# Second layer norm of a decoder layer: one early shift of all rows, VectorE takes the sums in a fixed order

## Chip, cores and metric

One core of one Trainium2 chip runs the whole kernel. The metric is device time in microseconds, from launch to end, median of three runs.

## The reference, cut to what matters

One layer of a hybrid decoder for 1024 prompt rows and 8 sample rows, 1032 rows of 1024 channels in all. The change lies in the last two lines, the feed-forward part and the layer norm behind it:

```python
x = layer_norm(ALPHA * x + (1 + g1) * m, ln1_g, ln1_b)
v = x * (1 + sc2) + sh2
hid = jnp.square(jax.nn.relu(v @ w_up))                      # 1024 -> 4096
x = layer_norm(ALPHA * x + (1 + g2) * (hid @ w_down), ln2_g, ln2_b)

def layer_norm(x, g, b):
    mu = x.mean(-1); var = ((x - mu) ** 2).mean(-1)
    return (x - mu) * rsqrt(var + LN_EPS) * g + b
```

## The kernel before, in words

Activations lie transposed: channels on the 128 partitions, in 8 row groups m = 0 to 7 (`x1[0]` to `x1[7]`), and the 1032 sequence positions along the columns. A layer norm therefore sums over partitions and over the 8 tiles. The sum over partitions is a matmul with a matrix of ones (`total`, L814 to L821), whose result stands on every partition and is evicted by ScalarE (ACT).

**Matmuls.** Every fp32 operand is split into a high and a low part (`split`, L202: ACT casts the high part, VectorE (DVE) subtracts for the low part). A `product` (L217) is, for each block of columns, three matmuls (L210: high x high, low x high, high x low) per 128 channels of the contraction, into one of four PSUM banks of tag mm, and then an evacuation by VectorE. The weight loads go through SP's queue (L146) into two buffers of tag raw, one weight ahead of use.

**Feed-forward.** The 4096 hidden channels are done in 5 chunks of four and then NFB = 2 chunks of six groups of 128. Each chunk first makes its hidden groups (`hidden`, L907 to L925): 24 matmuls per block of 344 columns, then per block ACT's relu, VectorE's square (L919), ACT's copy to the high part (L919) and VectorE's low part (L920). Then eight products with w_down are added into `x1[m]` by VectorE (`gate_add`, L761 to L768: one operation from PSUM, and for the block that holds the sample rows two narrow ones over 8 columns). All hidden groups read the same eight operand pairs `vh[k]`, `vl[k]`, which are the tiles `ks`; pair k = 4 was made with the tags ("xg", "xg") (L692), and tag xg has two buffers (L52). Pair 0 holds the two buffers of tag yc.

**Last chunk.** Its eight products run by column blocks LAST (L62): columns 640 to 1032, 256 to 640, 0 to 256. While the products of one block run, `ln2` takes the sums of the rows of that block: for row 0 a base is taken (its mean over 128 channels, L799 and L817), every row is shifted by it on VectorE (L825), squared on ACT (L806), the squares are summed on GpSimd (POOL, L810) and the rows on VectorE (L811). `finish` makes mean and variance (L837 to L851: two sums on PE, ln, exp and square on ACT, a Newton step on VectorE). The block before gets its output meanwhile: the shift by the mean on POOL (L825), the product with the reciprocal deviation on VectorE (L829), gain and bias on ACT (L986) or, for m = 3 to 5, on POOL (L984), and a DMA (L987). The last block's output has its own lines (L1024 to L1032).

**What sets the order.** A scheduler lays down each engine's instructions in one fixed sequence when the program is built. It takes what is ready by its own timing, and a new tile of a tag gets its buffer when all that reads the old tile in that buffer is done. Inside `manual_schedule` the instructions of the engines named keep the order in which they are written. Before, that holds for VectorE in the last block, and for VectorE and ACT behind it.

Of the kernel before, what the change touches and what calls it, by code (L numbers as in the profile page):

```python
# [11 lines left out]
F32R = mybir.dt.float32r  # L12
AF = mybir.ActivationFunctionType
ALU = mybir.AluOpType
# [3 lines left out]
P = 128  # L18
D = 1024
# [22 lines left out]
V_G2 = V_B1 + 8  # L42
V_B2 = V_G2 + 8
# [4 lines left out]
M_SH1, M_SC1, M_G1, M_SH2, M_SC2, M_G2 = (8 * i for i in range(6))  # L48
# [6 lines left out]
NFB = 2  # L55
# [4 lines left out]
BLOCKS = [(b * BW, (b + 1) * BW) for b in range(NB)]  # L60
LATER = [BLOCKS[2], BLOCKS[0], BLOCKS[1]]
LAST = [(640, T), (256, 640), (0, 256)]  # L62


def cols(ap, b):
    return ap[:, b[0]:b[1]]


def build(tc, ctx, a):
    nc = tc.nc  # L70
    dma = nc.sync.dma_start
    act = nc.scalar.activation
    ts = nc.vector.tensor_scalar
    tt = nc.vector.tensor_tensor
    stt = nc.vector.scalar_tensor_tensor
# [10 lines left out]
    def nm(s):  # L86
        uid[0] += 1
        return f"{s}_{uid[0]}"

    def slab(tag, dt=F32):  # L90
        return sp.tile([P, T], dt, tag=tag, name=nm(tag), bufs=SLOTS.get(tag, 1))

    def tmp(w=T, dt=F32):
        return sp.tile([P, w], dt, tag="t", name=nm("t"), bufs=5)

    def psm():
        return pm.tile([P, 512], F32, tag="mm", name=nm("mm"))

    def psa():
        return pq.tile([P, 512], F32, tag="ada", name=nm("ada"), bufs=1)  # L100

    def pss():
        return pq.tile([P, 512], F32, tag="sm", name=nm("sm"))
# [12 lines left out]
    eps = cp.tile([P, 1], F32, tag="eps", name="eps")  # L116
# [20 lines left out]
    def vc(base, j):  # L137
        return vec[:, base + j:base + j + 1]
# [49 lines left out]
    def prefetch():  # L188
        if order:
            key, raw = load_next()  # L190
            ahead.append((key, parts(*raw)))

    def weights(*key):
        if not ahead:
            prefetch()
        got, w = ahead.pop(0)
        assert got == key, (got, key)
        prefetch()
        return w
# [4 lines left out]
    def term(ps, w, x, i, n, b, which=range(3)):  # L204

        ko, xh, xl = x
        w_h, w_l = (t[:, ko * P:(ko + 1) * P] for t in w)
        for q in which:
            wt, xt = ((w_h, xh), (w_l, xh), (w_h, xl))[q]
            mm(ps[:, :b[1] - b[0]], wt, cols(xt, b), start=(i == 0 and q == 0), stop=(i == n - 1 and q == 2))  # L210

    def product(w, ks, evac, blocks=BLOCKS):
        for b in blocks:
            ps = psm()
            for i, x in enumerate(ks):
                term(ps, w, x, i, len(ks), b)
            evac(b, ps[:, :b[1] - b[0]])  # L217
            if not quiet[0]:
                next(background, None)
# [77 lines left out]
    with tc.manual_schedule(engines={mybir.EngineType.PE, mybir.EngineType.DVE, mybir.EngineType.Activation}):  # L297
        for q in range(4):
            ps = psa()
# [21 lines left out]
            for j, x in zip(js, xin):  # L321
                s, b = mod[:, M_SC1 + j], mod[:, M_SH1 + j]
# [3 lines left out]
                last = [nc.scalar.copy(uh[j], x)]  # L326
# [70 lines left out]
    for i in range(2):  # L397
        t, w, body, tail = pair0[i]
# [252 lines left out]
    def gated(j):  # L651
        gc = tmp()
        project(8 + j, lambda b, ps: nc.scalar.copy(cols(gc, b), ps))
        t, w, body, tail = padded(3)
        project(16 + j, lambda b, ps: tt(cols(body, b), ps, cols(gc, b), op=ALU.mult))
        r = convolve(t, w, 3, tail, sct4[:, j], lambda k: vc(V_CONVW + 8 * k, j), ncp[:, j], sct4[:, j])
        y = slab("yc")
        project(j, lambda b, ps: tt(cols(y, b), ps, cols(r, b), op=ALU.mult))
        return y
# [13 lines left out]
    y = gated(0)  # L673
    pre = ssd_pre(0)
    for c in range(NC):
# [7 lines left out]
        y = y1  # L683
# [22 lines left out]
    sums = []  # L706
    for g in range(2):
        for j in range(4 * g, 4 * g + 4):
# [9 lines left out]
            x, sq = xs[j][:, :TP], sz[:, :TP]  # L718
# [29 lines left out]
    x1 = [slab(f"U{m}") for m in range(8)]  # L748
    rones = cp.tile([P, P], F32R, tag="low", name="rones")
# [11 lines left out]
    def gate_add(dst, ps, row, m, b):  # L761

        lo, hi = b[0], min(b[1], TP)
        stt(dst[:, lo:hi], ps[:, :hi - lo], mod[:, row + m, 0:1], dst[:, lo:hi], op0=ALU.mult, op1=ALU.add)  # L764
        if b[1] > TP:
            gs = sp.tile([P, NS], F32, tag="gs", name=nm("gs"))
            tt(gs, ps[:, hi - lo:], mod[:, row + m, 1:9], op=ALU.mult)
            tt(dst[:, TP:T], dst[:, TP:T], gs, op=ALU.add)  # L768
# [18 lines left out]
    class Norm:  # L787
# [26 lines left out]
        def total(self, dst, srcs, n, b, bias=None, w=ones):  # L814
            pn = pss()[:, :b[1] - b[0]]
            for i, src in enumerate(srcs):
                mm(pn, w, src, start=(i == 0), stop=(i == len(srcs) - 1))  # L817
            if bias is None:
                act(cols(dst, b), pn, AF.Copy, scale=1.0 / n)
            else:  # L820
                act(cols(dst, b), pn, AF.Identity, scale=1.0 / n, bias=bias)  # L821
# [43 lines left out]
    ln1 = Norm(x1, ("st", "U14", "U15"))  # L865
# [58 lines left out]
    def hidden(i):  # L924
        w, evac, hl, _ = hidden_start(i)  # L925
        product(w, kv, evac)
        return hl
# [32 lines left out]
    for f in range(NFA):  # L960
        kh = [t[2] for t in two] if f == 0 else []
        kh += [hidden(4 * f + i) for i in range(len(kh), 4)]
        for mp in range(4):
            w = weights("wda", f, mp)
            for m in (2 * mp, 2 * mp + 1):
                product(w, [(4 * (m % 2) + i, h, l) for i, (h, l) in enumerate(kh)],
                        lambda b, ps: gate_add(x1[m], ps, M_G2, m, b))
    for f in range(NFB):
        kh = [hidden(4 * NFA + 6 * f + i) for i in range(6)]
        kf = [(i, h, l) for i, (h, l) in enumerate(kh)]  # L970
        if f < NFB - 1:
            for m in range(8):
                product(weights("wdb", f, m), kf, lambda b, ps: gate_add(x1[m], ps, M_G2, m, b))
            continue
        ln2 = Norm(x1, ("xg", "xg", "yc"))

        def output_start(m, b):
            ln2.shift(m, b, nc.gpsimd)
            ln2.scale(m, b)

        def output_end(m, b):
            x = cols(x1[m], b)
            if 2 < m < 6:
                nc.gpsimd.tensor_scalar(x, x, vc(V_G2, m), vc(V_B2, m), op0=ALU.mult, op1=ALU.add)  # L984
            else:
                act(x, x, AF.Identity, scale=vc(V_G2, m), bias=vc(V_B2, m))  # L986
            dma(a["o_y"][m, :, b[0]:b[1]], x)  # L987

        def output(m, b):
            output_start(m, b)  # L990
            output_end(m, b)

        wd = []

        def last_block(i):
            b, last = LAST[i], i == len(LAST) - 1
            for m in range(8):
                if i == 0:
                    wd.append(weights("wdb", f, m))
                product(wd[m], kf, lambda b, ps: gate_add(x1[m], ps, M_G2, m, b), (b,))  # L1000
                for k in ((), (0,), (1, 2))[m] if m < 3 else (m,):
                    ln2.add(k, b, last)
                if i and 2 < m < 6:
                    output(m - 3, LAST[i - 1])
            if not last:
                ln2.finish(b)
            if i:
                for m in range(3, 8):
                    output_start(m, LAST[i - 1])
                    if not last or m < 6:  # L1010
                        output_end(m, LAST[i - 1])

        for i in range(len(LAST) - 1):
            last_block(i)
        with tc.manual_schedule(engines={mybir.EngineType.DVE}):
            last_block(len(LAST) - 1)
        b = LAST[-1]
        w = b[1] - b[0]
        y = [tmp(4 * w).rearrange("p (m c) -> p m c", m=4) for i in range(2)]
        with tc.manual_schedule(engines={mybir.EngineType.DVE, mybir.EngineType.Activation}):  # L1020
            ln2.finish(b, (range(4), ()), range(4, 8), lambda: [output_end(m, LAST[-2]) for m in (6, 7)])
            for m in range(8):
                x, to = cols(x1[m], b), y[m // 4][:, m % 4]
                ln2.scale(m, b, nc.gpsimd if m > 5 else nc.vector)  # L1024
                if m > 5:
                    nc.gpsimd.tensor_scalar(to, x, vc(V_G2, m), vc(V_B2, m), op0=ALU.mult, op1=ALU.add)
                elif m == 3:
                    ts(to, x, vc(V_G2, m), vc(V_B2, m), op0=ALU.mult, op1=ALU.add)
                else:
                    act(to, x, AF.Identity, scale=vc(V_G2, m), bias=vc(V_B2, m))  # L1030
                if m % 2:
                    dma(a["o_y"][m - 1:m + 1, :, b[0]:b[1]].rearrange("m p c -> p m c"), y[m // 4][:, m % 4 - 1:m % 4 + 1])  # L1032

# [80 lines left out]
```

## Time and profile before

| | |
|---|---|
| median of three runs | 1598.09 us (1596.28 to 1599.17) |
| profiled execution, its own time | 1595.34 us |
| its span in the profile | 1593.6 us |
| mean granted clock | 0.992 |
| last feed-forward chunk's products | from 1497.72 us to 1572 us |

Times within the profile are microseconds from the span's start. PE is the matrix engine, DVE is VectorE, ACT ScalarE, POOL GpSimd. A row of the timeline gives start, length, engine, line of the code, operation, output and inputs, shape and count, and in brackets how long the engine was idle before and what ended that. Several instructions in a row of the same kind are merged; the lengths of neighbours overlap a little, as an operation's start is reported before the one ahead of it is through.

### The profile page before, as it was taken

Reading aid. Unit: us, or ns where it says so; the run is one execution under the profiler, and the core shown is the slowest. Engines: PE = TensorE matmul, PEld = TensorE weight load, DVE = VectorE, ACT = ScalarE, POOL = GpSimd, SP = SyncE. Lnnn points to the kernel's source line nnn. Section 1 sums busy time; section 2 is a strip of 40 time slices with the busy share of each in tenths; the row PEclk is TensorE's granted clock in tenths of the full one; section 3 lists DMA queues with packets and bytes.
Section 4 is the critical chain, followed back from the end, with each engine's and each line's share of the span. In section 5 each row is a group of like instructions: output and inputs, shape, how many; then the busy total and the mean of one; then the engine's idle time right before and its main releaser. Section 6 shows DMA issues by size and latency. Waiting matters only on the chain.

```text
span 1593.6 us, 24010 instructions
## 1 busy us (share of the span) xinstructions
PE 1545.2 (97%) x10057; PEld 1492.0 (94%) x10057; DVE 877.3 (55%) x1629; ACT 524.2 (33%) x803; POOL 214.1 (13%) x212
## 2 busy tenths in 40 slices
PE   7999979999999999999999999999999999999994
PEld 4899878999999999999999999999999999999994
DVE  4576556767666652545897434434343433333488
ACT  2453322333333343713477122121312113113334
POOL 0017880000000001100241000000000000000076
PEclk9999989999999999999999999999999999999998
DMA  9434443333333322512311111111111111111211
GB/s 362 124 110 135 150 162 113 120 120 119 120 106 104 111 104 70 200 53 66 106 58 62 41 40 54 41 53 41 53 42 52 42 52 43 41 54 46 70 41 66
DMA packets 49628, 141.44 MB, mean 89 GB/s; under 512 B 5736, under 2 KB 14696, under 8 KB 49520
## 3 DMA queue, kind: packets, MB, share of 16 engines
q1 hardware_dynamic: 49520, 139.91, 26.8%
q8 instruction: 79, 1.29, 0.3%
q14 instruction: 29, 0.24, 0.1%
HBM read 126.33 MB, written 13.56 MB: 88 GB/s over the span
## 4 chain that ended last, share of the span: by engine, by line
PE 85%; DVE 5%; POOL 5%; DMA 2%; issue 1%; ACT 1%; SPq 0%; ACTq 0%; DVEq 0%; POOLq 0%
PE mm L210 78%; POOL s L526 1%; PE ada L229 1%; POOL w L528 1%; POOL w L525 1%; PE sm L626 1%; PE sm L618 1%; DMA s<-in_ssm 1%; DVE U L825 1%; POOL s L523 1%; PE sm L613 1%; PE sm L817 1%; PE sm L648 1%; DVE U L829 1%; DMA o_ssm<-s 1%
## 5 line engine op out<-in xcount | busy, mean ns | idle before, releaser
L210 PE MATMUL mm<-U,whi 128*128 128x344 f32 x3058 | 780.5, 324 | 0.0
L210 PEld LDWEIGHTS mm<-U,whi 128*128 128x128 f32 x3058 | 538.8, 189 | 17.7 <-issue 13.6
L210 PE MATMUL mm<-U,wlo 128*128 128x344 f32 x1529 | 490.1, 323 | 0.0
L202 ACT CAST whi<-raw 128x1024 fp32r<-128x1024 f32 (+1 forms) x124 | 127.6, 1030 | 525.7 <-PE mm L210 517.5
L210 PEld LDWEIGHTS mm<-U,wlo 128*128 128x128 f32 x1529 | 288.1, 189 | 3.1 <-issue 2.9
L764 DVE SCALAR_TENSOR_TENSOR U<-mm,mod,U 128x344 f32<-128x344 f32 (+3 forms) x216 | 122.5, 570 | 203.4 <-PE mm L210 203.3
L210 PE MATMUL mm<-S,whi 128*128 128x344 f32 (+3 forms) x912 | 233.0, 320 | 0.0
L202 DVE TENSOR_TENSOR wlo<-raw,whi 128x1024 fp32r<-128x1024 f32 (+1 forms) x124 | 150.9, 1217 | 127.2 <-ACT whi L202 126.8
L210 PEld LDWEIGHTS mm<-S,whi 128*128 128x128 f32 x912 | 160.6, 188 | 0.1
L210 PE MATMUL mm<-S,wlo 128*128 128x344 f32 (+3 forms) x456 | 145.0, 319 | 0.0
L210 PE MATMUL mm<-C,whi 128*128 128x344 f32 x516 | 143.0, 320 | 0.0
L810 POOL TENSOR_TENSOR yc<-yc,t 128x392 f32<-128x392 f32 (+2 forms) x20 | 21.2, 1062 | 681.2 <-ACT t L806 680.7
L919 DVE TENSOR_TENSOR t<-t 128x344 f32<-128x344 f32 x96 | 49.3, 515 | 93.6 <-ACT t L919 93.6
L210 PEld LDWEIGHTS mm<-C,whi 128*128 128x128 f32 x516 | 92.9, 188 | 0.1
L210 PEld LDWEIGHTS mm<-S,wlo 128*128 128x128 f32 x456 | 85.6, 188 | 0.1
L210 PE MATMUL mm<-C,wlo 128*128 128x344 f32 x258 | 82.5, 320 | 0.0
L210 PE MATMUL mm<-G,whi 128*128 128x344 f32 x258 | 82.1, 321 | 0.1
L210 PE MATMUL mm<-xg,whi 128*128 128x344 f32 x258 | 82.0, 320 | 0.0
L369 DVE SCALAR_TENSOR_TENSOR t<-t,vec,t 128x1064 f32<-128x1064 f32 (+1 forms) x52 | 75.1, 1452 | 4.4 <-ACT t L367 3.5
L919 ACT ACTIVATE t<-mm 128x344 f32<-128x344 f32 x96 | 43.7, 456 | 97.0 <-PE mm L210 97.0
L210 PE MATMUL mm<-yc,whi 128*128 128x344 f32 x210 | 66.8, 322 | 0.0
L920 DVE TENSOR_TENSOR S<-t,S 128x344 fp32r<-128x344 f32 x66 | 33.9, 516 | 29.5 <-ACT S L919 29.3
(353 smaller groups left out, 2143.0 us busy)
## 6 DMA issues: line engine op xcount, KB each, us to landing
raw<-in_win SPq DMA_DIRECT2D x44, 512.0 KB, 3.7
aw<-in_wada SPq DMA_DIRECT2D x33, 512.0 KB, 3.9
raw<-in_wup SPq DMA_DIRECT2D x32, 512.0 KB, 3.5
raw<-in_wout SPq DMA_DIRECT2D x24, 512.0 KB, 3.5
raw<-in_wda SPq DMA_DIRECT2D x20, 512.0 KB, 3.6
G<-acd SPq DMA_DIRECT2D x16, 512.0 KB, 3.8
raw<-in_wdb SPq DMA_DIRECT2D x16, 384.0 KB, 3.1
S<-in_xT SPq DMA_DIRECT2D x8, 516.0 KB, 11.2
```

Of the source, the lines that this page charges most:

```text
L202: return nc.scalar.copy(thi, src), tt(tlo, src, thi, op=ALU.subtract)
L210: mm(ps[:, :b[1] - b[0]], wt, cols(xt, b), start=(i == 0 and q == 0), stop=(i == n - 1 and q == 2))
L229: mm(ps[32 * g:32 * g + 32, :256], cs[:, 2 * kp + k2, :], w[:, c:c + 256], start=(kp == 0), stop=(kp == KD // 2 - 1), tile_position=(0, 32 ...
L369: stt(r, t[:, k:k + n], wt(k), r, op0=ALU.mult, op1=ALU.add)
L523: ptt(s0, s0, ddx[:, j, NS:][:, bs].unsqueeze(2).to_broadcast([P, HB, NST]), op=ALU.mult)
L525: ptt(w0, wide["b"], xdt.unsqueeze(2).to_broadcast([P, HB, NST]), op=ALU.mult)
L526: ptt(s0, s0, w0, op=ALU.add)
L528: ptt(w0, s0, wide["c"], op=ALU.mult)
L764: stt(dst[:, lo:hi], ps[:, :hi - lo], mod[:, row + m, 0:1], dst[:, lo:hi], op0=ALU.mult, op1=ALU.add)
L810: nc.gpsimd.tensor_tensor(q, q, w, op=ALU.add)
L919: return [lambda: act(x, ps, AF.Relu), lambda: tt(x, x, x, op=ALU.mult), lambda: nc.scalar.copy(xh, x), lambda: tt(xl, x, xh, op=ALU.subtr ...
L920: lambda: tt(xl, x, xh, op=ALU.subtract)]
```

## The change

All rows are shifted once, by the mean over the first 128 channels, ahead of the last chunk, instead of in each block. A layer norm does not change when one number is taken from all channels of a position. The three sums of the base are taken from `x1[0]` as it is then. `base` is a tile of tag xg, as are `mean` and `rsum`; `qsum` has tag yc. In the last chunk POOL no longer sums squares nor shifts rows: VectorE does both, and POOL keeps gain and bias for m = 2 and 5. The squares of the last rows 6 and 7 and row 7 itself go into PE's sums directly. All VectorE work of the chunk, the weight splits among it, keeps the written order: per product its gate_add, the two sums of that row, then one centre and one scaling of the block before (for m = 0 two centres and the variance, for m = 1 the Newton step, one centre and two scalings). ACT is no longer ordered by hand.

```diff
+    def shift_rows():
+        near, base = tmp(dt=F32R), slab("xg")
+        nc.scalar.copy(near, x1[0])
+        for b in BLOCKS:
+            ln1.total(base, (cols(near, b),), P, b, w=rones)
+        for m in range(8):
+            tt(x1[m], x1[m], base, op=ALU.subtract)
+
     for f in range(NFB):
+        if f == NFB - 1:
+            shift_rows()
         kh = [hidden(4 * NFA + 6 * f + i) for i in range(6)]
...
-        ln2 = Norm(x1, ("xg", "xg", "yc"))
...
+        total = ln1.total
+        mean, rsum, qsum = (slab(t) for t in ("xg", "xg", "yc"))
+        def sums(m, b, last):
+            x, q, s = cols(x1[m], b), cols(qsum, b), cols(rsum, b)
+            if m == 0:
+                act(q, x, AF.Square)
+                return
+            w = cols(tmp(), b)
+            act(w, x, AF.Square)
+            if last and m > 5:
+                rest[1].append(w)
             else:
-                act(x, x, AF.Identity, scale=vc(V_G2, m), bias=vc(V_B2, m))
-            dma(a["o_y"][m, :, b[0]:b[1]], x)
+                tt(q, q, w, op=ALU.add)
+            if last and m == 7:
+                rest[0].append(x)
+            else:
+                tt(s, s if m > 1 else cols(x1[0], b), x, op=ALU.add)
+        rest = [], []
+        def moments(b):
+            mu, s, q = cols(mean, b), cols(rsum, b), cols(qsum, b)
+            total(mean, (s, *rest[0]), D, b)
+            act(s, mu, AF.Square)
+            total(qsum, (q, *rest[1]), D, b, eps)
...
+        def center(m, b):
+            tt(cols(x1[m], b), cols(x1[m], b), cols(mean, b), op=ALU.subtract)
+        def affine(m, b, to):
+            tt(cols(x1[m], b), cols(x1[m], b), cols(qsum, b), op=ALU.mult)
+            if m % 3 == 2:
+                nc.gpsimd.tensor_scalar(to, cols(x1[m], b), vc(V_G2, m), vc(V_B2, m), op0=ALU.mult, op1=ALU.add)
+            else:
+                act(to, cols(x1[m], b), AF.Identity, scale=vc(V_G2, m), bias=vc(V_B2, m))
...
+        early_c = {0: (0, 1), 1: (2,), 2: (3,), 3: (4,), 4: (5,), 5: (6,), 6: (7,)}
+        early_o = {1: (0, 1), 2: (2,), 3: (3,), 4: (4,), 5: (5,), 6: (6,)}
         with tc.manual_schedule(engines={mybir.EngineType.DVE}):
-            last_block(len(LAST) - 1)
...
+            for i, b in enumerate(LAST):
+                last, before = i == len(LAST) - 1, LAST[i - 1]
+                for m in range(8):
+                    if i == 0:
+                        wd.append(weights("wdb", f, m))
+                    product(wd[m], kf, lambda b, ps: gate_add(x1[m], ps, M_G2, m, b), (b,))
+                    if i and m == 0:
+                        for k in early_c[0]:
+                            center(k, before)
+                        w = variance(before)
+                    sums(m, b, last)
+                    if i and m == 1:
+                        newton(before, w)
+                    if i:
+                        for k in early_c.get(m, ()) if m else ():
+                            center(k, before)
+                        for k in early_o.get(m, ()):
+                            output(k, before)
+                if i and not last:
+                    output(7, before)
+                moments(b)
+            y = [tmp(4 * (b[1] - b[0])).rearrange("p (m c) -> p m c", m=4) for i in range(2)]
+            for m in range(4):
+                center(m, b)
+            w = variance(b)
+            output(7, before)
+            for m in range(4, 6):
+                center(m, b)
+            newton(b, w)
+            for m in (0, 1, 2, 3, 4, 5, 6, 7):
                 if m > 5:
...
+                    center(m, b)
+                affine(m, b, y[m // 4][:, m % 4])
```

## Rows read from the trace of the kernel before

**Rows 1.** The page, busy time of engines (part 1) and a DMA issue (part 6).
```profile
PE 1545.2 (97%) x10057; PEld 1492.0 (94%) x10057; DVE 877.3 (55%) x1629; ACT 524.2 (33%) x803; POOL 214.1 (13%) x212
...
raw<-in_wdb SPq DMA_DIRECT2D x16, 384.0 KB, 3.1
```
**Rows 2.** Windows: stretch, length, busy PE, PEld, DVE, ACT, POOL, clock, DMA share, GB/s.
```profile
1540.00:1560.00 20.00, 17.62 (x113) 16.86 (x111) 18.02 (x29) 8.14 (x16) 13.88 (x13) 1.00 0.22 81
...
1576.00:1580.00 4.00, 3.67 (x8) 2.25 (x8) 3.97 (x8) 1.35 (x4) 2.77 (x3) 0.57 0.13 49
```
**Rows 3.** Timeline of PE, last hidden block and last chunk.
```profile
1496.13 0.32 PE L210 MATMUL mm<-xg,whi 128*128 128x344 f32 x1
...
1497.72 0.34 PE L210 MATMUL mm<-S,whi 128*128 128x392 f32 x1
...
1500.22 0.51 PE L210 MATMUL mm<-S,whi 128*128 128x392 f32 x2
...
1506.83 1.77 PE L210 MATMUL mm<-S,U 128*128 128x392 f32 x9
...
1557.43 0.91 PE L817 MATMUL sm<-xg,ones 128*128 128x384 f32 x2 [2.38 <-DVE xg L811]
...
1562.56 1.59 PE L210 MATMUL mm<-S,U 128*128 128x256 f32 x12
...
1576.33 1.09 PE L817 MATMUL sm<-xg,ones 128*128 128x256 f32 x2 [4.35 <-ACT t L806]
```
**Rows 4.** Timeline of DVE, second and third block of the last chunk.
```profile
1525.61 0.61 DVE L764 SCALAR_TENSOR_TENSOR U<-mm,mod,U 128x384 f32<-128x384 f32 x1
...
1538.01 4.45 DVE L829 TENSOR_TENSOR U<-U,yc 128x392 f32<-128x392 f32 x6
...
1543.86 2.27 DVE L825 TENSOR_TENSOR U<-U,xg 128x384 f32<-128x384 f32 x4
...
1557.29 0.87 DVE L764 SCALAR_TENSOR_TENSOR U<-mm,mod,U 128x256 f32<-128x256 f32 x2
...
1570.36 0.43 DVE L811 TENSOR_TENSOR xg<-xg,U 128x256 f32<-128x256 f32 x1
...
1576.10 0.48 DVE L764 SCALAR_TENSOR_TENSOR U<-mm,mod,U 128x256 f32<-128x256 f32 x1
```
**Rows 5.** Timeline of ACT, last chunk.
```profile
1527.61 0.53 ACT L806 ACTIVATE t<-U 128x392 f32<-128x392 f32 x1 [1.89 <-DVE U L825]
...
1530.27 0.50 ACT L819 ACTIVATE xg<-sm 128x392 f32<-128x392 f32 x1 [2.13 <-PE sm L817]
...
1577.47 0.42 ACT L806 ACTIVATE t<-U 128x256 f32<-128x256 f32 x1 [1.24 <-DVE U L825]
...
1589.06 1.09 ACT L1030 ACTIVATE t<-U,vec 128x256 f32<-128x256 f32 x2 [0.59 <-DVE U L829]
```
**Rows 6.** Timeline of DVE, hidden groups and first block of the last chunk.
```profile
1442.24 1.23 DVE L202 TENSOR_TENSOR wlo<-raw,whi 128x1024 fp32r<-128x1024 f32 x1 [2.84 <-ACT whi L202]
...
1498.83 0.96 DVE L202 TENSOR_TENSOR wlo<-raw,whi 128x768 fp32r<-128x768 f32 x1 [0.19 <-ACT whi L202]
...
1500.77 0.52 DVE L920 TENSOR_TENSOR S<-t,S 128x344 fp32r<-128x344 f32 x1 [0.55 <-ACT S L919]
...
1505.54 0.61 DVE L764 SCALAR_TENSOR_TENSOR U<-mm,mod,U 128x384 f32<-128x384 f32 x1
...
1506.26 0.17 DVE L768 TENSOR_TENSOR U<-U,gs 128x8 f32<-128x8 f32 x1
...
1513.50 1.51 DVE L825 TENSOR_TENSOR U<-U,xg 128x392 f32<-128x392 f32 x3
1514.93 0.16 DVE L768 TENSOR_TENSOR U<-U,gs 128x8 f32<-128x8 f32 x1
```
**Rows 7.** Timeline of POOL, output of the block before and its gain and bias.
```profile
1530.85 9.28 POOL L825 TENSOR_TENSOR U<-U,xg 128x392 f32<-128x392 f32 x8 [1.53 <-ACT xg L819]
...
1541.61 4.90 POOL L984 TENSOR_SCALAR U<-U,vec 128x392 f32<-128x392 f32 x3 [1.49 <-DVE U L829]
```

More of the change, by code (lines that the diff above doesn't have):

```diff
@@ L974, in build @@
             continue
-        ln2 = Norm(x1, ("xg", "xg", "yc"))
[L977 to L984, printed above, removed]
-            else:
-                act(x, x, AF.Identity, scale=vc(V_G2, m), bias=vc(V_B2, m))
-            dma(a["o_y"][m, :, b[0]:b[1]], x)
+        total = ln1.total
@@ new lines, in build, with variance @@
+        rest = [], []
[4 more added lines that the diff above has]
+            total(qsum, (q, *rest[1]), D, b, eps)
+        def variance(b):
+            s, q, w = cols(rsum, b), cols(qsum, b), cols(tmp(), b)
+            tt(s, q, s, op=ALU.subtract)
+            act(q, s, AF.Ln)
+            act(q, q, AF.Exp, scale=-0.5)
+            act(w, q, AF.Square)
+            return w
@@ new lines, in newton @@
+        def newton(b, w):
+            s, q = cols(rsum, b), cols(qsum, b)
+            stt(w, w, -0.5, s, op0=ALU.mult, op1=ALU.mult)
+            stt(q, w, 1.5, q, op0=ALU.add, op1=ALU.mult)
+        def center(m, b):
[6 more added lines that the diff above has]
+                act(to, cols(x1[m], b), AF.Identity, scale=vc(V_G2, m), bias=vc(V_B2, m))
@@ L989, in output @@
         def output(m, b):
-            output_start(m, b)
-            output_end(m, b)
+            affine(m, b, cols(x1[m], b))
+            dma(a["o_y"][m, :, b[0]:b[1]], cols(x1[m], b))
         wd = []
[L995 to L1011, printed above, removed]
@@ L1013, in build @@
-        for i in range(len(LAST) - 1):
-            last_block(i)
-        with tc.manual_schedule(engines={mybir.EngineType.DVE}):
-            last_block(len(LAST) - 1)
[L1017 to L1024, printed above, removed]
-                if m > 5:
[L1026 to L1030, printed above, removed]
+        early_c = {0: (0, 1), 1: (2,), 2: (3,), 3: (4,), 4: (5,), 5: (6,), 6: (7,)}
```

## Prediction

> **What bounds the kernel now.** I read the page first: PE is busy 97% of the span [rows 1], so almost everywhere only matmul time counts. The change, however, touches the end, and there the windows read differently: from 1540 to 1560 us VectorE (DVE) is busy 18.0 of 20 us and PE 17.6 [rows 2]. The PE timeline says when the roles change. The products of the last feed-forward chunk begin at 1497.72; PE waits 2.38 us for a VectorE sum before 1557.43, and idles 4.35 us between the last product, at 1572.0, and the last sums at 1576.33 [rows 3]. The last gate_add ends at 1576.10 + 0.48 = 1576.6 [rows 4]. The other 17.0 us to the span's end, 1593.6, hold no product. So three things set the end: when PE may start the chunk, how fast VectorE's queue gets to the last gate_add, and the tail behind it.
>
> **Term 1, the shift of whole rows: +7.6 us.** The eight subtracts are written ahead of the last hidden products, and there VectorE has room. But their operand `base` takes a buffer of tag xg. There are two, and both hold the fifth operand pair of every hidden product: PE still reads xg at 1496.13 to 1496.45 [rows 3], in the last hidden block. `base` can't be written before that, so the copy of row 0 and its three sums run early, but the three evictions wait. One costs 0.50 at 392 columns [rows 5], about 0.46 at 344: 1496.5 + 1.4 = 1497.9. Then come eight subtracts over 1032 columns. A 1024-column subtract takes 1.23, of which some 0.08 overlaps the next [rows 6]: 8 x 1.15 = 9.2, to 1507.1.
>
> Queued behind them are the last hidden block's two VectorE steps (square, low half). The order of a queue is fixed when the program is built, and among ready work what is written earlier seems to go first: three per-row shifts run at 1513.50 ahead of a narrow add of a later product at 1514.93 [rows 6]. So square, ScalarE's copy and low half run at 1507.1, 1507.7 and 1508.4 (a weight split slips between), to 1508.9. Before, they ended at 1501.3 [rows 6]. Who waits is PE: the first product needs that hidden block from its sixth operand on, about 1500.4 [rows 3]. Nor can it go to a third product, as it does now, since the fixed VectorE order puts that split behind the first gate_add. The delay is 1508.9 - 1501.3 = 7.6. Bounds: 0 if the subtracts found free time, 9.2 if none. I take 7.6 since the buffer row is plain and the priority row points the same way.
>
> **Term 2, the clock: +1.8 us.** After 4.35 us of idle PE ran 1576 to 1580 at a granted clock of 0.57, so largely at 1.2 of 2.4 GHz [rows 2, 3]. A stall of over 7 us should do the same: 3.7 us of work at half speed [rows 2] lose 1.8. Bounds 0 and 3.7.
>
> **Term 3, the queue through three blocks: +2.0 us.** Nothing is shifted per block now, POOL adds no squares and shifts no rows, and VectorE does all of it in a fixed order. Prices without POOL beside it: two-operand ops 0.48 at 392 and 384 columns (three in 1.51) [rows 6] and 0.35 at 256 (0.43 with overlap); gate_add 0.53 and 0.40 [rows 4]. The new wait: each sum of squares stands right behind its gate_add and needs ScalarE's square of that row, 0.53 or 0.42 [rows 5] plus two hand-overs, so VectorE stands 0.6 or 0.5 us with the plain sum, a centre, a scaling and the next gate_add queued behind.
> First block, a row: gate_add with its narrow ops 0.9 (1505.54 to 1506.43) [rows 6], wait 0.6, two sums 0.96, a split 0.88: 3.35, against PE's 18 x 0.179 = 3.2 (nine matmuls in 1.77) [rows 3]. Eight rows lose at most 1 us; before, the last gate_add of this block came at 1525.61 [rows 4], 2 us behind PE. I take 0. The moved weight loads keep up: each is issued on SP when a split frees one of two buffers, and lands 3.1 us later [rows 1], so a load, its copy and its split fit in two rows.
> Second block: without the stall its first gate_add starts at 1497.7 + 8 x 3.2 + 3.1 (its own product) + 1.3 (two sums on PE, two records of one 0.91 at 384) [rows 3] = 1527.7. Then eight gate_adds 4.2, seven waits 4.3, fourteen sums 6.7, eight centres, variance and Newton 5.4, eight scalings 3.8, the mean's round trip 1.6, squares late behind a scaling on ScalarE 5 x 0.3 = 1.5 (an estimate) and 1.5 in which VectorE waits for PE: 29, to 1556.7. Before it was 1557.29 [rows 4]: -0.6.
> Third block (256 columns, centres and scalings of 384): eight gate_adds 3.2, six waits 3.1, eleven sums 3.9, eight centres, variance and Newton 5.4, seven scalings 3.3, the mean 1.5, late squares 1.5: 21.9, to 1578.6. A row costs 2.9 against PE's 18 x 0.119 = 2.14 [rows 3], so VectorE sets this block. Before: 1576.6. Hence +2.0; bounds -2.5 (row at PE's pace) and +4.
>
> POOL is where a price is not plain. While it did adds and subtracts (eight took 9.28), VectorE's scalings took 0.74 rather than 0.48; while it did three scale-and-bias ops of 1.63, four VectorE subtracts took 2.27, 0.55 each [rows 4, 7]. Six such ops stay on POOL, so I add nothing for them. The Trainium skill (SBUF — State Buffer, SBUF: two separate sides) says otherwise: a VectorE op with two SBUF inputs and a POOL op that reads SBUF exclude each other for the whole instruction. By it the sum would be that of rival 4; 0.55 against 1.63 does not look like it, so the sum goes by the row.
>
> **Term 4, the tail: -2.6 us.** The last row is no longer shifted before its square. From the last gate_add: last matmul of the sum on a slow PE and hand-overs 1.1 (two records 1.09) [rows 3], eviction 0.4, square of the mean and second eviction 1.4, four centres in between, variance 0.8: 3.7. Then ln, exp and square with one output of the block before among them 2.1, Newton 0.9, eight scalings and two centres 3.6, the last scale-and-bias 0.6: 10.9. Behind that, as before, 1593.6 - 1590.15 = 3.45 [rows 5]. 14.4 against 17.0. Bounds -4 and 0. The output DMAs are as many on SP as before, 20, and still not what it waits for.
>
> **Sum.** 7.6 + 1.8 + 2.0 - 2.6 = +8.8 on the profiled execution, whose 1595.34 us is the span and 1.74: 1604.1. The median shown, 1598.09, lies 2.75 above that execution, which would give 1606.9. I give 1605.5, between the two.
>
> **Rivals.**
> 1. Faster. The rows are out of the way early and VectorE keeps PE's pace in the third block: terms 1 and 2 vanish, and six rows win 0.75 each: 2.0 - 4.5 - 2.6 = -5.1, 1590.2 to 1593.0. Place: the eight subtracts; it decides at whether they stand before 1496.5. For it: between the hidden steps VectorE has time, 2.84 us idle ahead of 1442.24 [rows 6], and POOL's collisions go. Against: xg is in use. Chance 0.17.
> 2. Interleaved. The last hidden steps go ahead of the remaining subtracts. PE then has no long wait and no slow clock, and the subtracts fill the six waits of 0.6 in the first block: of 9.2 us at most 9.2 - 3.6 = 5.6 stays, and nothing if PE's lead over VectorE covers it. Half of that is 2.8: 2.8 + 2.0 - 2.6 = +2.2, 1597.5 to 1600.3. For it speaks that VectorE would not stand still in the first block, against it the order at 1513.50 [rows 6]. Chance 0.15.
> 3. The subtracts are hidden ahead of 1496.5, for instance because the buffer is free after all, and the rest is as summed: 2.0 - 2.6 = -0.6, 1594.7 to 1597.5. Chance 0.08.
> 4. Besides the forecast, each of the four scale-and-bias ops that POOL does while VectorE's queue sets the pace holds one VectorE op for 1.63 rather than 0.48 [rows 6, 7]: 4 x 1.15 = 4.6 more, 1608.7 to 1611.5. The rule above is what speaks for it, the 0.55 against. Chance 0.04.
> The forecast keeps 0.56.
>
> **How the numbers follow.** A measurement of this kernel can tell 0.2%, 3.2 us: faster is under 1594.9, slower over 1601.3. Slower is forecast and rival 4, 0.60; within is rivals 2 and 3, 0.23; faster is rival 1, 0.17. The forecast's own range is 1599.4 to 1610.9: down from 1604.1 by the clock's 1.8 and by half the way to the lower bounds of terms 3 and 4, 2.2 and 0.7; up from 1606.9 by half the way to the upper bounds of all four, 4. The range goes down over rivals 2 and 3 to 1594.5 and leaves out most of rival 1 and the top: 1594.5 to 1610.
>
> **What would show it.** Right: eight VectorE subtracts of 1032 columns in one row from 1498 to 1507; PE waiting over 6 us in the first product, then a clock near 0.5; one gate_add per 2.9 us in the last block; 14 to 15 us from the last gate_add to the end. Wrong: subtracts at 1440 to 1490 would undo terms 1 and 2; PE without a wait at 1500 would mean rival 2 or 3; a last block at 2.2 a row would undo term 3.

## The result and the profile after

The changed kernel takes **1610.76 us** (median of 4 runs, 1610.08 to 1612.10), the kernel before 1597.93 us beside it: a ratio of 1.0082, 95% interval 1.0064 to 1.0099, 12.8 us slower. That is the side that was forecast, at 1605.5 us, and 0.8 us above the top of the range. (Ratios below are likewise to the kernel before, run beside each.) The profiled execution took 1611.34 us with a span of 1609.5, against 1593.6 before.

First the page of the changed kernel, busy time of the engines, to be held against [rows 1]: POOL does 44 instructions and 49 us less, VectorE (DVE) has 24 instructions more and is 2.7 us less busy. The engine that took on work is not busier, since its operations are shorter now that POOL adds no squares and shifts no rows beside them (a plain sum of the last chunk takes 527 ns on the mean of 17, 645 before). What the change costs is therefore waiting.

```profile
PE 1550.4 (96%) x10058; PEld 1495.1 (93%) x10058; DVE 874.6 (54%) x1653; ACT 525.0 (33%) x805; POOL 165.2 (10%) x168
```

**The start of the last chunk.** Timeline of VectorE of the changed kernel, from the subtracts to the chunk's first gate_add (start, length, instruction, idle time before and what ended it):

```profile
1499.60 9.24 DVE L975 TENSOR_TENSOR U<-U,xg 128x1032 f32<-128x1032 f32 x8 [1.31 <-ACT xg L819]
1508.76 0.95 DVE L202 TENSOR_TENSOR U<-raw,U 128x768 fp32r<-128x768 f32 x1
1509.63 0.95 DVE L202 TENSOR_TENSOR wlo<-raw,whi 128x768 fp32r<-128x768 f32 x1
1510.49 0.51 DVE L919 TENSOR_TENSOR t<-t 128x344 f32<-128x344 f32 x1
1511.55 0.52 DVE L920 TENSOR_TENSOR S<-t,S 128x344 fp32r<-128x344 f32 x1 [0.54 <-ACT S L919]
1516.88 0.62 DVE L764 SCALAR_TENSOR_TENSOR U<-mm,mod,U 128x384 f32<-128x384 f32 x1 [4.81 <-PE mm L210]
```

The eight subtracts of whole rows stand in one row and wait for ScalarE's eviction into xg. Behind them come two weight splits and only then the last hidden block's square and low half, which ended at 1501.3 before [rows 6] and end at 1512.07 now. ScalarE and TensorE show why, and what it does:

```profile
1498.41 1.16 ACT L819 ACTIVATE xg<-sm 128x344 f32<-128x344 f32 x3 [0.67 <-PE mm L210]
```

```profile
1431.20 0.63 PE L817 MATMUL sm<-t,rones 128*128 128x344 f32 x3
...
1498.21 0.32 PE L210 MATMUL mm<-xg,whi 128*128 128x344 f32 x1
...
1502.65 0.34 PE L210 MATMUL mm<-S,U 128*128 128x392 f32 x1
1509.76 2.00 PE L210 MATMUL mm<-S,U 128*128 128x392 f32 x5 [6.77 <-DVE U L202]
```

The sums of row 0 are done 67 us earlier, but their evictions wait until TensorE has read xg for the last time, near 1498.5 (the ends of matmuls are modelled; the first eviction is recorded at 1498.41). Then TensorE stands for 6.77 us, until the weight split of the third product is through, and the windows of the changed kernel (columns as in [rows 2]) show the clock behind that wait:

```profile
1504.00:1508.00 4.00, 0.00 (x0) 0.00 (x0) 4.00 (x5) 0.00 (x0) 0.00 (x0) 0.96 0.00 0
1508.00:1512.00 4.00, 2.24 (x7) 2.24 (x8) 3.46 (x5) 0.48 (x1) 0.00 (x0) 0.50 0.33 98
1512.00:1516.00 4.00, 4.00 (x18) 4.00 (x17) 0.07 (x1) 1.67 (x2) 0.00 (x0) 0.69 0.31 102
```

**The three blocks.** Timeline of VectorE again: two rows of the first block, the first gate_add of the second block and what follows it, two rows of the third, and the wait of the tail:

```profile
1521.88 0.61 DVE L764 SCALAR_TENSOR_TENSOR U<-mm,mod,U 128x384 f32<-128x384 f32 x1
...
1523.36 0.57 DVE L1000 TENSOR_TENSOR yc<-yc,t 128x392 f32<-128x392 f32 x1 [0.60 <-ACT t L996]
...
1525.19 0.61 DVE L764 SCALAR_TENSOR_TENSOR U<-mm,mod,U 128x384 f32<-128x384 f32 x1
...
1541.47 0.61 DVE L764 SCALAR_TENSOR_TENSOR U<-mm,mod,U 128x384 f32<-128x384 f32 x1
1546.46 1.04 DVE L1029 TENSOR_TENSOR U<-U,xg 128x392 f32<-128x392 f32 x2 [4.37 <-ACT xg L819]
...
1588.92 0.48 DVE L764 SCALAR_TENSOR_TENSOR U<-mm,mod,U 128x256 f32<-128x256 f32 x1
1590.09 0.43 DVE L1000 TENSOR_TENSOR yc<-yc,t 128x256 f32<-128x256 f32 x1 [0.69 <-ACT t L996]
...
1591.70 0.48 DVE L764 SCALAR_TENSOR_TENSOR U<-mm,mod,U 128x256 f32<-128x256 f32 x1
...
1597.09 1.43 DVE L1029 TENSOR_TENSOR U<-U,xg 128x256 f32<-128x256 f32 x4 [2.94 <-ACT xg L819]
```

A row costs 3.31 us in the first block and 2.78 in the third. In the rows shown, VectorE stands 0.6 to 0.7 us ahead of the sum of squares (L1000). The waits of VectorE from 1497 to the end (total, times, longest) put that first:

```profile
DVE yc L1000 <- ACT t L996: 14.4, 19, 1.6
DVE U L1029 <- ACT xg L819: 8.4, 3, 4.4
DVE U L764 <- PE mm L210: 6.7, 2, 4.8
```

The wait of 4.37 us for the mean has its cause on TensorE's queue: the sums' last input, a VectorE add, is done at 1541.55, and they run behind a whole product of the next block:

```profile
1541.92 1.21 PE L210 MATMUL mm<-S,U 128*128 128x384 f32 x6
...
1544.01 1.22 PE L210 MATMUL mm<-S,U 128*128 128x384 f32 x6
1545.07 0.82 PE L817 MATMUL sm<-xg,ones 128*128 128x392 f32 x2
```

**One scale for all kernels.** The profiled executions differ already ahead of the change. So times below are counted in each trace from the start of the last gate_add of the chunk before (the one of 336 columns; 1429.77 before, 1431.40 after) to the start of a block's first gate_add and to the end of the span:

| kernel | 1st block | 2nd block | 3rd block | last gate_add | end |
|---|---|---|---|---|---|
| before | 75.8 | 98.3 | 127.5 | 146.3 | 163.8 |
| after | 85.5 | 110.1 | 140.8 | 162.3 | 178.1 |
| after, own buffer (e1) | 75.9 | 100.7 | 131.5 | 152.9 | 168.8 |
| before, early shift (e2) | 76.9 | 97.5 | 123.0 | 140.2 | 157.7 |
| subtracts written later (e3) | 85.0 | 109.8 | 140.5 | 162.0 | 177.4 |
| subtracts behind low half (e5) | 81.3 | 105.6 | 136.4 | 157.8 | 173.7 |
| busy in the wait (e8) | 84.6 | 109.3 | 140.0 | 161.6 | 177.3 |
| e1, squares last (e4) | 75.9 | 99.1 | 124.8 | 146.0 | 161.5 |
| e4, mean a row later (e6) | 75.9 | 99.1 | 125.2 | 146.8 | 162.7 |
| e1, squares on POOL (e7) | 75.9 | 97.4 | 124.1 | 143.4 | 158.8 |
| e1, sums first on TensorE (e9) | 75.9 | 100.6 | 128.7 | 150.8 | 166.5 |
| e7, sums first on TensorE (e10) | 75.9 | 97.4 | 123.0 | 141.5 | 155.8 |

Each row is one profiled execution. Of 14.3 us at the end (178.1 - 163.8), 9.7 are there at the first gate_add, and 4.6 come behind it.

### The profile page after: what moved, and what is told of

The parts are those of the page before. It is cut to its first block, busy times and chain, and to the rows that moved or that the text cites. A ratio compares the mean times of both kernels' runs of the same rounds, so it can differ in the third digit from the quotient of the medians.

```text
span 1609.5 us, 23963 instructions
## 1 busy us (share of the span) xinstructions
PE 1550.4 (96%) x10058; PEld 1495.1 (93%) x10058; DVE 874.6 (54%) x1653; ACT 525.0 (33%) x805; POOL 165.2 (10%) x168
## 4 chain that ended last, share of the span: by engine, by line
PE 84%; DVE 5%; POOL 5%; DMA 2%; ACT 2%; issue 2%; SPq 0%; POOLq 0%; ACTq 0%; DVEq 0%
PE mm L210 77%; POOL s L526 1%; POOL w L528 1%; PE ada L229 1%; POOL w L525 1%; POOL s L523 1%; PE sm L626 1%; PE sm L618 1%; PE sm L613 1%; PE sm L817 1%; PE sm L648 1%; DVE U L1032 1%; DMA s<-in_ssm 1%; DVE U L1029 1%; DMA yc<-in_wada 1%
## 5 line engine op out<-in xcount | busy, mean ns | idle before, releaser
L202 DVE TENSOR_TENSOR wlo<-raw,whi 128x1024 fp32r<-128x1024 f32 (+1 forms) x124 | 151.6, 1223 | 127.5 <-ACT whi L202 127.2
L919 ACT ACTIVATE t<-mm 128x344 f32<-128x344 f32 x96 | 43.7, 456 | 97.4 <-PE mm L210 97.4
L919 ACT CAST S<-t 128x344 fp32r<-128x344 f32 x66 | 31.6, 480 | 57.3 <-DVE t L919 57.1
```

The lines of the kernel that those rows point to most:

```text
L202: return nc.scalar.copy(thi, src), tt(tlo, src, thi, op=ALU.subtract)
L919: return [lambda: act(x, ps, AF.Relu), lambda: tt(x, x, x, op=ALU.mult), lambda: nc.scalar.copy(xh, x), lambda: tt(xl, x, xh, op=ALU.subtr ...
```

## Experiments

### The buffer of the shift (e1)

```
-        near, base = tmp(dt=F32R), slab("xg")
+        near, base = tmp(dt=F32R), tmp()
```

> The changed kernel, but the base of the early shift gets a buffer of its own kind (tag t, free then) instead of tag xg. Theory (the shift waits for the xg buffer, and stands ahead of the last hidden block's steps): the eight subtracts run near 1432 to 1442 us, PE has no wait over 1 us when the last chunk's products begin and no stretch below full clock there; the time falls by the 11.3 us that the first block lost, to about 1599.5 us (1598 to 1601.5). Rival (the fixed order on VectorE is what costs): the time stays above 1606 us.

Measured: 1601.25 us, ratio 1.0027 (1.0017 to 1.0037), 9.5 us less than the changed kernel's median. On VectorE's timeline of this kernel the subtracts stand 66 us earlier on the common scale, right behind the chunk before:

```profile
1432.61 9.23 DVE L975 TENSOR_TENSOR U<-U,t 128x1032 f32<-128x1032 f32 x8
```

The first gate_add comes at 75.9, as before the change. So the stall is the buffer's alone, 9.3 us at the end (178.1 - 168.8). But 5.0 us against before are left.

### The early shift without the rest (e2)

The kernel before, with the shift of whole rows into a free buffer and no shift by blocks; the sums of squares stay on POOL and the order stays as it was.

```
+        near, base = tmp(dt=F32R), tmp()
...
-        ln2 = Norm(x1, ("xg", "xg", "yc"))
+        ln2 = Norm(x1, ("xg", "xg", "yc"), True)
```

> The kernel before, with the early shift alone (base in tag t), and without the shift of each block; sums of squares stay on POOL and the order stays as it was. Theory (VectorE's queue sets the last two blocks, and the per-block shifts are a part of it): about 1595 us (1592 to 1597). Rival (the rows' way through the sums is no bound, PE and the tail are): 1597 to 1599 us, as before.

Measured: 1590.11 us, ratio 0.9961 (0.9948 to 0.9973), below what was expected. The early shift is worth 6.8 us; the changed kernel loses it in the buffer and, as e7 below shows, in the sums of squares that VectorE took on.

### What put the subtracts ahead of the low half (e3, e5)

e3 writes the subtracts behind the last hidden block; e5 ties each of them behind its last low half besides.

```
     kh = [hidden(4 * NFA + 6 * f + i) for i in range(6)]
+    if f == NFB - 1:
+        for m in range(8):
+            tt(x1[m], x1[m], base, op=ALU.subtract)                          # e3
+            after(tt(x1[m], x1[m], base, op=ALU.subtract), low_halves[-1])   # e5
```

> The changed kernel with base still in tag xg, but the eight subtracts are written behind the last hidden products instead of ahead of them. Theory (what is written earlier goes first, so that PE's wait comes from the place and not from the amount of the subtracts): the last hidden block's steps go first, PE waits less than 1.5 us there, the clock stays full, and the subtracts lie between the gate_adds: about 1603.5 us (1601 to 1606). Rival (the 9.2 us of VectorE time are the cost wherever they lie in the first block): 1608 to 1611 us.

> The changed kernel with base still in tag xg, but each of the eight subtracts is held behind the last hidden block's low half on VectorE's queue. What is told apart is the place (PE's wait for the last hidden block, and the slow clock behind it) from the amount (9.2 us of VectorE time in the first block, wherever it lies). Measured so far against the kernel before: changed kernel +12.8 us, own buffer +4.4. Theory of the place alone: PE goes on through products 1 to 3 while VectorE subtracts, no wait over 1.5 us, about +4.4 to +6 us. Theory of both: PE comes through three products and then waits some 4 us for the fourth weight and for banks, as the first gate_add comes 7 us later than with the own buffer; clock mostly full; +8 to +10 us. Amount alone: +12 to +13 us.

Measured: e3 1609.81 us, 1.0079 (1.0066 to 1.0093), which lies in its rival's range, but does not test that rival, as the subtracts did not move; e5 1607.35 us, 1.0064 (1.0052 to 1.0077), 10.8 us above before, between two of its theories. Written later, the subtracts still go first, as VectorE's timeline of e3 shows:

```profile
1497.69 9.24 DVE L982 TENSOR_TENSOR U<-U,xg 128x1032 f32<-128x1032 f32 x8 [1.31 <-ACT xg L819]
...
1509.63 0.52 DVE L920 TENSOR_TENSOR S<-t,S 128x344 fp32r<-128x344 f32 x1 [0.54 <-ACT S L919]
```

So their place in the program does not decide it; that the scheduler had them ready before the square is the reading left, and no run tested it. In e5 the low half does go first:

```profile
1503.60 0.52 DVE L922 TENSOR_TENSOR S<-t,S 128x344 fp32r<-128x344 f32 x1 [0.55 <-ACT S L921]
1504.03 9.23 DVE L984 TENSOR_TENSOR U<-U,xg 128x1032 f32<-128x1032 f32 x8
```

Its end comes at 173.7: 4.9 us above e1 and 4.4 below after. Of the 9.3 us, 4.4 are the place ahead of the low half, and 4.9 remain with the subtracts directly behind it, since the first gate_adds wait behind them. (TensorE's clock fell in e5 too, to 0.68 from 1516 to 1520. A run with the subtracts between the gate_adds is missing.) TensorE's waits of e5 show a smaller and later one, for the first gate_add, in place of the 6.8 for a split:

```profile
PE mm L210 <- DVE gs L767: 3.7, 1, 3.7
PE mm L210 <- DVE U L202: 0.6, 1, 0.6
```

### The clock (e8)

```
         tt(x1[m], x1[m], base, op=ALU.subtract)
+        if m < 7:
+            mm(pss()[:, :392], ones, x1[m][:, :392], start=True, stop=True)
```

> The changed kernel, and in PE's wait one fp32 matmul with 392 columns behind each of the first seven subtracts, whose sum nothing reads: added work that only keeps PE busy. Theory (some 2.4 us of the loss are the clock, which falls in the wait and comes back 5 us after it): the granted clock stays at or near 1.00 from 1508 to 1516, and the time is 1.5 to 3 us below that of the changed kernel, +10 to +11.3 us against the kernel before. Rival (VectorE's queue would hold the first block up all the same): +12 to +13.5 us.

Measured: 1609.46 us, 1.0082 (1.0068 to 1.0095): the ratio of the changed kernel, and at +12.9 us the rival's range. The windows of this kernel show full clock where the changed kernel has 0.50 and 0.69:

```profile
1508.00:1512.00 4.00, 3.65 (x20) 3.66 (x21) 2.10 (x4) 1.25 (x2) 0.00 (x0) 1.00 0.55 176
1512.00:1516.00 4.00, 3.81 (x21) 3.27 (x19) 1.40 (x4) 1.41 (x3) 0.00 (x0) 1.00 0.05 21
```

In the traces the first gate_add gains 0.9 us and the end 0.8. That is near the scatter: VectorE's low half ends 80.67 us behind the mark in this kernel, in the changed one and in e3, and VectorE then waits for the first product 3.92, 4.81 and 4.35 us. So the slow clock costs 0.4 to 0.9 us at the first gate_add, and in the medians nothing that can be told.

### VectorE's sums of squares (e4, e7)

On e1: e4 puts each sum of squares behind the plain sum, the centre and the scaling of its row; e7 gives it to POOL.

```
-                tt(q, q, w, op=ALU.add)
+                squares.append(lambda: tt(q, q, w, op=ALU.add))      # e4
+                nc.gpsimd.tensor_tensor(q, q, w, op=ALU.add)         # e7
...
+                    while squares:                                   # e4
+                        squares.pop()()
```

> As e1_own_buffer, and on VectorE the sum of squares of a row stands behind the plain sum, the centre and the scaling instead of right behind the gate_add. Theory (VectorE stands 0.5 to 0.7 us at every row for ScalarE's square, and in the third block that is on the path): one gate_add per 2.2 to 2.4 us in the third block instead of 2.8, and 2.5 us less than e1_own_buffer, about 1597 us (1595.5 to 1598.5). Rival (these waits are covered by PE): the same time as e1_own_buffer within 1 us.

> As e1_own_buffer, but the sums of squares are again added on POOL (19 operations), all else on VectorE in the same order. Theory (what costs in the fixed order is that VectorE stands for ScalarE's square, and this wait goes with the sum of squares): as e4_squares_last within 2 us, 0 to 3 us below the kernel before, with VectorE's additions slowed from 0.48 to about 0.6 while POOL adds. Rival (taking the sums away from POOL is what helps, since POOL's additions hold VectorE's up): slower than e1_own_buffer, more than 4.4 us above the kernel before.

Measured: e4 1594.57 us, 0.9980 (0.9971 to 0.9989), 6.7 us below e1 where 2.5 were expected; e7 1590.37 us, 0.9961 (0.9949 to 0.9974), 10.9 below e1, and 6.2 below before where 0 to 3 were expected. In e4 the line `L1000 <- ACT` is gone from VectorE's waits, and another grew, from 8.5 us in e1:

```profile
DVE U L1030 <- ACT xg L819: 10.5, 3, 4.1
```

On the common scale the same work without its wait gives 7.3 us at the end, the work taken away as well gives 10.0. Most of what VectorE's squares cost was waiting. And e7 is level with e2 (0.9961 both): the fixed order and the shift by the mean on VectorE, which e7 keeps, cost nothing that the ratios show. What the change loses besides the buffer are these nineteen operations.

### Where the mean waits (e6, e9, e10)

e6 (on e4) uses the mean one product later; e9 (on e1) and e10 (on e7) put the next block's products from the second row on behind the sums on TensorE's queue.

```
-        early_c = {0: (0, 1), 1: (2,), 2: (3,), 3: (4,), 4: (5,), 5: (6,), 6: (7,)}
+        early_c = {1: (0, 1), 2: (2,), 3: (3, 4), 4: (5,), 5: (6,), 6: (7,)}         # e6
...
+                first = term(ps, w, x, i, len(ks), b)                                # e9, e10
+                if i == 0 and behind_sums:
+                    after(first, last_sum[0])
```

> As e4_squares_last, and in the second and third block the first two centres and the variance stand behind the gate_add of the second product instead of the first, the Newton step and the outputs one product later. Theory (VectorE stands 4 to 6 us at each block's start for the sum and the mean, which PE's queue holds behind products, and in the third block that is on the path): the first three gate_adds of the third block come 2 to 3 us closer together, 2 to 4 us less than e4_squares_last, that is 4 to 6.5 us below the kernel before. Rival (the lag is made good by the queue anyway, PE being the bound): within 1 us of e4_squares_last, 2 to 3 us below the kernel before.

> The changed kernel with a free buffer for the shift's operand (1601.25 us when it ran alone), and the products from the second row on in the second and third block put behind the two sums of the block before on TensorE's queue. In the changed kernel those sums ran at 1545.07 behind a whole product, though their last input was done at 1541.55, and VectorE waited 4.37 us for the mean. Theory (that product is what makes the mean late, and the mean is what the queue waits for): the wait falls to about 1.3 us, the second row's gate_add then waits for its product, which is pushed back by the sums' 1.6 us, so 1.2 us are won at each of two blocks: 1598.9 us (1597.5 to 1600). Rival A (the whole 3.1 us of each wait count, the product is not missed): 1595 us. Rival B (the place of the sums costs nothing, VectorE's own work sets the pace): 1601 us.

> The same order of the sums on TensorE's queue, and the sums of squares on POOL instead of VectorE (1590.37 us with the latter alone; there VectorE waited 6.4 us for the mean in three goes, the tail's included, and 9.5 us for products). Theory: 0.5 us is won at each of two blocks, since the second row's gate_add then waits for its product: 1589.4 us (1588 to 1590.5). Rival A (each wait for the mean counts whole): 1587 us. Rival B: no change, 1590.4 us, or worse, as the product pushed back is what VectorE waits for: 1592 us.

Measured: e6 1595.36 us, 0.9991 (0.9982 to 1.0000), no gain over e4, as its rival said. It does not settle why: VectorE's wait for the mean falls only from 10.5 to 9.1 us, and 3.7 us of waits for ScalarE's squares, gone in e4, are back. e9 1598.86 us, 1.0016 (1.0007 to 1.0026), where 1598.9 was expected. The number came, its parts did not: the second block is 2.6 us shorter than in e1 and the third 0.6 longer, not 1.2 shorter each, as VectorE's wait for the mean in the third block of e1 is only 1.1 us. e10 1588.78 us, 0.9953 (0.9940 to 0.9965): the lowest median, 1.6 us below e7's, but its interval overlaps those of e2 and e7. VectorE's timeline of e9 in the second block shows why only part of the wait is won:

```profile
1532.71 1.04 DVE L1037 TENSOR_TENSOR U<-U,xg 128x392 f32<-128x392 f32 x2 [1.02 <-ACT xg L827]
...
1536.00 0.62 DVE L772 SCALAR_TENSOR_TENSOR U<-mm,mod,U 128x384 f32<-128x384 f32 x1 [1.68 <-PE mm L211]
```

The wait for the mean falls from 4.38 in e1 to 1.02, and 1.68 of it comes back as a wait for the product that now stands behind the sums.

## Why the prediction was right in its side and short in its size

**Term 1 and term 2, 9.4 us forecast: 9.3 measured** (after against e1, at the end). The step on the buffer held (e1): the subtracts start at 1499.60, which is 1498.0 on the clock of before (the execution runs 1.63 late), where 1497.9 was worked out. Three smaller steps did not. Two splits slipped in, not one, so the low half is late by 9.15 us on the common scale (1512.07 - 1431.40 against 1501.29 - 1429.77), not 7.6. What is written earlier did not decide the order (e3). And TensorE did go to a third product, whose split ended its wait. The clock fell as forecast, 0.50 and 0.69, but was worth 0.4 to 0.9 at the first gate_add, not 1.8. The parts missed in opposite directions, so the good sum is partly luck.

**Term 3, the queue through three blocks, +2.0 us forecast, is the step that failed**: e1 against before gives 6.6 us up to the last gate_add (152.9 - 146.3).
- First block, taken as 0: +2.3 (24.8 against 22.5 from its first gate_add to the next block's). VectorE's rows were sized well, 3.35 against 3.31 measured, and kept the pace of before: in e1 VectorE is through with seven of them 20.2 us after the first gate_add, and the eighth gate_add came 20.1 us after the first before. What is new is a wait of 2.01 us there for the eighth product (1.92 in the changed kernel). So the 0 was wrong on TensorE's side: the prediction asked whether the moved weight loads keep up with VectorE's rows, and not what a later split does to the order of TensorE's products. The split of the eighth product's weights (output G) now has its place in the written order. Before, VectorE made it at 1512.63, and TensorE's product followed at 1520.43:

```profile
1512.63 0.96 DVE L202 TENSOR_TENSOR G<-raw,G 128x768 fp32r<-128x768 f32 x1 [0.92 <-ACT G L202]
```

```profile
1520.43 1.24 PE L210 MATMUL mm<-S,G 128*128 128x392 f32 x6
```

In e1 the split comes 7.4 us later on the common scale, and TensorE's sequence has a product of the second block (384 columns) ahead of the eighth. VectorE and TensorE of e1:

```profile
1520.60 0.95 DVE L202 TENSOR_TENSOR G<-raw,G 128x768 fp32r<-128x768 f32 x1
...
1528.57 0.62 DVE L764 SCALAR_TENSOR_TENSOR U<-mm,mod,U 128x384 f32<-128x384 f32 x1 [2.01 <-PE mm L210]
```

```profile
1522.18 0.34 PE L210 MATMUL mm<-S,whi 128*128 128x384 f32 x1
...
1525.35 1.05 PE L210 MATMUL mm<-S,G 128*128 128x392 f32 x5
```

In e7, whose rows are shorter, the split comes 3.8 us earlier than in e1, the eighth product follows the seventh again, and the block is 3.3 us shorter. That the late split is why TensorE's sequence changed is argued, as no run moved it alone.
- Second block, forecast 29: 30.8. The mean's trip was put at 1.6, and VectorE's wait for it alone is 4.4, since the sums stand behind a product. e9 takes 2.6 us off this block.
- Third block, forecast 21.9 to the end of its last gate_add: 21.9. Here the row of 2.9 (2.78 measured) held.

**Term 4, the tail, -2.6 forecast: -1.6** (15.9 against 17.5, e1 against before). One pair of TensorE's records was counted between the last gate_add and the mean's eviction. There are five pairs, at a granted clock of 0.50 from 1592 to 1596; the eviction waits for the fourth, and they run to 1597.06:

```profile
1592.97 1.19 PE L817 MATMUL sm<-xg,ones 128*128 128x256 f32 x2 [6.45 <-DVE xg L1004]
...
1596.47 0.59 PE L817 MATMUL sm<-t,ones 128*128 128x256 f32 x2
```

The mean is evicted 2.9 us after the last gate_add's end, not 1.5.

**The sum.** On the profiled execution +8.8 was forecast and +16.0 measured. Of the 7.2 between, 1.6 stood there before the changed stretch began, which is put down to scatter between executions (the mark lies between 1429.18 and 1432.24 in these traces), and 5.6 are terms 3 and 4 (6.6 - 1.6 = 5.0 against 2.0 - 2.6 = -0.6).

**The rivals.** Rival 1's and 3's place, subtracts ahead of 1496.5, is e1. It costs 5.0 us there, not the -5.1 or -0.6 worked out, because terms 3 and 4 were short. Rival 2 is nearest in e5, where 4.9 of the stall stayed against 2.8 forecast, but no run interleaved the subtracts with the gate_adds. The measured 1610.76 lies in rival 4's range, by another cause; its 4.6 did not come: POOL's four operations in these blocks take 0.67 each, not the 1.63 of [rows 7], and start beside a gate_add; only one VectorE operation behind them is stretched, at 1592.21, where an add over 256 columns takes 0.61 rather than 0.42.

## What to carry to other kernels

A step that is written early runs early only if the buffer it writes is free: look for the last reader of that buffer, here 67 us later, before any gain is counted. In an order fixed by hand, an operation that needs another engine's answer goes last in its group, so that the wait lies beside work (7.3 us here for nineteen operations). And an order fixed by hand holds all that the engine does: look for what another engine needs out of it, here a weight split, and not only at the time that a row takes.

## What the runs showed that was not expected

Which of POOL and VectorE is stretched depends on who stands in the other's way. Timelines of e7, POOL first, then VectorE:

```profile
1564.28 1.61 POOL L1034 TENSOR_SCALAR U<-U,vec 128x384 f32<-128x384 f32 x1
1565.86 1.62 POOL L1000 TENSOR_TENSOR yc<-yc,t 128x256 f32<-128x256 f32 x2
...
1570.80 0.66 POOL L1034 TENSOR_SCALAR U<-U,vec 128x384 f32<-128x384 f32 x1 [0.52 <-DVE U L1032]
```

```profile
1564.50 0.55 DVE L1029 TENSOR_TENSOR U<-U,xg 128x384 f32<-128x384 f32 x1
1564.97 0.55 DVE L1032 TENSOR_TENSOR U<-U,yc 128x384 f32<-128x384 f32 x1
1565.44 0.47 DVE L764 SCALAR_TENSOR_TENSOR U<-mm,mod,U 128x256 f32<-128x256 f32 x1
1565.94 0.94 DVE L1004 TENSOR_TENSOR xg<-xg,U 128x256 f32<-128x256 f32 x1
1566.81 1.09 DVE L1029 TENSOR_TENSOR U<-U,xg 128x384 f32<-128x384 f32 x1
```

POOL's scale-and-bias at 1564.28 has VectorE operations with two SBUF inputs beside it until the gate_add at 1565.44; it takes 1.61 and leaves the two shown at 0.55, as without POOL; one that starts beside a gate_add takes 0.66. Two POOL adds in a row stretch VectorE's next two to 0.94 and 1.09. The Trainium skill (SBUF — State Buffer, SBUF: two separate sides) states that such a VectorE operation and a POOL operation that reads SBUF exclude each other for a whole instruction, whichever starts first. These rows can be read so: POOL waits out a VectorE queue without gaps and runs beside the gate_add, one of whose operands is in PSUM. Then the prediction's argument against the rule, VectorE's 0.55 beside POOL's 1.63 [rows 4, 7], would show only who lost, and the 1.63 that rival 4 took as the price would be for the most part POOL's own waiting. No run tried the rule by itself.
